# One in eight of the expert weights' low parts is computed on GpSimd instead of VectorE

## The chip, the cores and the metric

The kernel runs on one core of a Trainium2 chip. A core has TensorE (PE in the profile; PEld is its weight load), VectorE (DVE), ScalarE (ACT), GpSimd (POOL) and SyncE (SP), each with a queue of its own that it works off in order, and 16 DMA engines that move data between device memory and the core's on-chip memory SBUF. TensorE writes its results to eight banks of PSUM. The metric is the device time of one launch in microseconds (us); before the change it was 1439.66, the median of 3 runs from 1438.84 to 1440.0.

## The reference

Two transformer layers over 256 tokens of width 1024, in float32. Layer 0 is attention and a dense feed-forward block. Layer 1 is attention and a mixture of eight experts, of which each token uses two:

```python
def moe_swiglu(h, w_router, w1, w3, w2):
    t = h.reshape(b * s, d)
    logits = jnp.dot(t, w_router).astype(jnp.float32)
    top_val, top_idx = lax.top_k(logits, TOP_K)
    top_w = jax.nn.softmax(top_val, axis=-1)
    gates = jnp.einsum('tk,tke->te', top_w,
                       jax.nn.one_hot(top_idx, N_EXPERTS, dtype=jnp.float32)).astype(h.dtype)
    def expert(args):
        e_w1, e_w3, e_w2, g = args
        hid = jax.nn.silu(t @ e_w1) * (t @ e_w3)
        return (hid @ e_w2) * g[:, None]
    y = jnp.sum(lax.map(expert, (w1, w3, w2, gates.T)), axis=0)
```

For each expert e_w1 and e_w3 are 1024 x 3584 and e_w2 is 3584 x 1024. The change is in the experts.

## The kernel before

**Three products instead of one.** The matmuls here take float32r, not float32. So every weight w is split into a high part `wh` (w written as float32r) and a low part `wl` (w minus `wh`), and the tokens likewise; `mm3` (L174) then issues three matmuls into one bank: x_h·wh (L176), x_h·wl (L177), x_l·wh (L178). In the experts the tokens' parts `eh, el` lie in memory that the profile names `oh_t` and `ol_t`.

**The stream of weights.** All weights are loaded in one fixed order (`jobs`) by SP, 1 MB a tile (`raw`), into a ring of tile slots; a slot's next load starts when the slot's readers are done. `stream` (L138) hands the weights out. It takes half a tile at a time, 128 x 1024 numbers, called a *piece* below. ScalarE writes `wh` (L154), VectorE then writes `wl` from `raw` and `wh` (L155). The pool `split` (L52) has four buffers for `wh` and four for `wl`, so the two engines can be at most four pieces ahead of TensorE. A piece feeds six matmuls of 512 columns.

**The experts.** Tokens of an expert are gathered to at most 128 rows. An expert's hidden width is worked off in seven *blocks* of 512. A block takes four pieces of e_w1 into one bank, four pieces of e_w3 into another, and four pieces of e_w2 that go with the block before (L943 to L952). `gate_mul` (L584) makes `nat` = silu(w1 result) on ScalarE (L586), times the w3 result on VectorE (L587); `hid_t` (L592) turns `nat` by four transposes (L598) and splits it on ScalarE and VectorE (L182, L183). Each expert thus has 84 pieces, 7 `nat` and 7 splits of the turned hidden values. VectorE's queue holds all of them in one order, and so does ScalarE's.

**What GpSimd does before.** In the experts it only issues transfers, in order: four indirect DMAs that scatter the tokens to `xs_d` by expert (L828, during the first expert), a load of the next expert's tokens (L848) and a store of each expert's result (L855), and near the end some fetches (L836).

**Order.** The program is written in the order of the code below; a scheduler with its own timing model then sets the order within each engine's queue. It moves matmuls past others that it expects to wait.

Of the kernel before, what the change touches and what calls it, by code (L numbers as in the profile page):

```python
# [10 lines left out]
F32 = mybir.dt.float32  # L11
# [10 lines left out]
NC = D // P  # L22
# [15 lines left out]
WARM = 6  # L38
WARMS = 1, 1, 1
MIDDLE = 6  # L40
FAR = 4096
PUMPS = (7, 7), (7, 7), (7, 7), (7, 7), (2, 3), (2, 3), (1, 3), (2, 2), (2, 2)

# [2 lines left out]
def block_kernel(ctx: ExitStack, tc: tile.TileContext, x, w_qkv, w_o, mixer_norm, ffn_norm,  # L46
                 rel_bias, w1, w3, w2, router, e_w1, e_w3, e_w2, final_norm, onehot, out):
    nc = tc.nc
# [57 lines left out]
    def behind(*pairs):  # L106

        for a, b in pairs:
            if b is not None:
                tc.add_manual_dep(a.ins, b.ins.name,  # L110
                                  mybir.DependencyInfo(mybir.DependencyClass.NoSync,
                                                       mybir.DependencyReason.DATA),
                                  reason="issue order")

    held, recent = [None, None], [None]
# [18 lines left out]
    def load_ahead():  # L134
        while n_loaded[0] < min(n_used[0] + len(slots_of), len(jobs)):
            load_next()

    def stream(n, g=None, hold=(None, None), free=2):  # L138


        got = taken = 0
        while got < n:
            load_ahead()
            t = loaded[n_used[0]]
            _, nk, fn = jobs[n_used[0]]
            n_used[0] += 1
            k = min(nk, HALF // fn)
            for c0 in range(0, nk, k):
                wh = split.tile([P, HALF], F32R, name="wh")
                wl = split.tile([P, HALF], F32R, name="wl")  # L150
                m = k * fn
                src = t[:, c0 * fn:c0 * fn + m]
                if g is None:
                    i0 = nc.scalar.activation(wh[:, :m], src, AF.Copy)  # L154
                    i1 = nc.vector.tensor_sub(wl[:, :m], src, wh[:, :m].bitcast(F32))  # L155
                    if taken >= free:
                        behind((i0, hold[0]), (i1, hold[1]))
                else:
                    for c in range(k):
                        cs = slice(c * fn, (c + 1) * fn)  # L160
                        gc = gcol[:, g, got + c0 + c:got + c0 + c + 1]
                        i0 = nc.scalar.activation(wh[:, cs], src[:, cs], AF.Copy, scale=gc)  # L162
                        i1 = nc.vector.scalar_tensor_tensor(  # L163
                            wl[:, cs], src[:, cs], gc, wh[:, cs].bitcast(F32), op0=ALU.mult,
                            op1=ALU.subtract)
                        if taken >= free:
                            behind((i0, hold[0]), (i1, hold[1]))
                recent[0] = i0
                taken += 1
                for c in range(k):  # L170
                    yield wh[:, c * fn:(c + 1) * fn], wl[:, c * fn:(c + 1) * fn]
            got += nk
        assert got == n
# [116 lines left out]
    def norm_t(b, n, rms_too=True):  # L290
        for i in range(2):
            i0, i1 = split_out(turn(b, i),
                               xh[b][:, 4 * i:4 * i + 4].rearrange("p c t -> p (c t)"),
                               xl[b][:, 4 * i:4 * i + 4].rearrange("p c t -> p (c t)"))
        if rms_too:
            behind((rnorm(b, n), i0))
        return i0, i1
# [361 lines left out]
    hold = [norm_t(b, 0, False) for b in range(NB)]  # L659
# [4 lines left out]
    hold = hold[2:]  # L664
# [21 lines left out]
    def logits(b, after, between=None):  # L686
        lps = bank[0][:, b * NE:(b + 1) * NE]
        for c in range(NC):
            if c == MIDDLE and between:
                i0 = between()  # L690
# [125 lines left out]
    def send():  # L816

        nc.gpsimd.iota(rank, pattern=[[0, NB], [P, NE]], base=-1, channel_multiplier=0,
                       allow_small_or_imprecise_dtypes=True)
        nc.vector.tensor_scalar(place, slot, float(P), float(FAR), op0=ALU.is_gt, op1=ALU.mult)  # L820
        nc.vector.tensor_add(place, place, slot)
# [114 lines left out]
    for e in range(NE):  # L936
        for i, (f0, n) in enumerate(ecs):
            b1, b3 = (5, 6) if k % 2 == 0 else (3, 4)
            k += 1
            for bk in (b1, b3):  # L940
                if bk == b3:
                    held[:] = None, None
                for c, w in enumerate(stream(NC, hold=held)):  # L943
                    _, last = mm3(bank[bk], (eh[:, c], el[:, c]), w, c == 0, c == NC - 1)
                if pend is not None and bk == b1:
                    hT = hid_t(pend[1], FC, bank[pend[2]], *hts)
            if i == len(ecs) - 1 and e + 1 < NE:
                turn_x(xr, (2, 7), last)
            t = gate_mul(ep.tile([P, FC], F32, name="nat"), bank[b1], bank[b3], n)
            if pend is not None:  # L950
                for j, w in enumerate(stream(4)):
                    down(y, hT, j, w, pend[0] == 0, pend[0] == len(ecs) - 1)  # L952
            pend = (i, t, b1)
            if i == 0:
                if e:
                    store_y(e - 1)
                else:
                    gates()
                    send()

                    cps = bank[2]
                    for b in range(NB):
                        nc.tensor.matmul(cps[:, :NE], ones, sel[:, b], start=b == 0,
                                         stop=b == NB - 1)
                    most = mp.tile([P, 1], F32, name="most")
                    nc.vector.tensor_reduce(most, cps[:, :NE], axis=mybir.AxisListType.X,
                                            op=ALU.max)
                    most_i = mp.tile([P, 1], mybir.dt.int32, name="most_i")
                    nc.vector.tensor_copy(most_i, most)  # L969
                    nc.vector.tensor_scalar(pos2, slot, -float(P), None, op0=ALU.add)  # L970
            if i == 1 and e + 1 < NE:
                xr = load_x(e + 1)
            if e == NE - 1:
                if i == 0:
                    for b in range(NB):
                        mark(e, b)
                    done = slots(e)
                elif i == 2:
                    came = fetch(0, 0), fetch(0, 1)
                elif i == 3:  # L980
                    add_rows(0, came)
                    came = fetch(1, 0), fetch(1, 1)
                elif i == 4:
                    add_rows(1, came)
# [81 lines left out]
    for half in range(2):  # L1066
# [3 lines left out]
        i0, i1 = scatter(done, (half,), hts if half else ys)  # L1070
# [5 lines left out]
    for b in range(NB):  # L1076
# [3 lines left out]
        i1 = nc.vector.scalar_tensor_tensor(ms, ss[:, b, 1:2], 1.0 / D, ms, op0=ALU.mult,  # L1080
                                            op1=ALU.add)
# [49 lines left out]
```

## Time and profile before

| | |
|---|---|
| median of the runs | 1439.66 us |
| the profiled execution | 1440.46 us |
| its span on the core | 1438.7 us |
| TensorE busy | 1420.6 us (99%) |
| VectorE busy | 1170.3 us (81%) |
| ScalarE busy | 1009.7 us (70%) |
| GpSimd busy | 49.7 us (3%) |
| the 710 `wl` of L155 on VectorE | 834.1 us, 1221 ns each |
| the 710 `wh` of L154 on ScalarE | 724.7 us, 1056 ns each |

The experts fill the profile from about 457 us to 1424 us. Shares over the whole span mix stages: in the slices of the experts VectorE is at 9 tenths, in those of attention at 5 to 7. A busy TensorE is a modelled number (its matmuls are pipelined), so the start-to-start distance of matmuls tells more than its busy share. Idle time of an engine costs something only where another engine then waits for it.

### The profile page before, as it was taken

How to read it: one execution, taken by the hardware profiler on the slowest of the kernel's cores; microseconds unless marked ns; L12 is line 12 of the kernel's file. 1: busy time of each engine (PE TensorE's matmuls, PEld its weight loads, DVE VectorE, ACT ScalarE, POOL GpSimd, SP SyncE). 2: the span in 40 equal slices, each digit the busy share in tenths (PEclk: the TensorE clock that was granted, in tenths of full speed). 3: DMA queues.
4: the chain of work that ended last, by engine and by line, in shares of the span. 5: the costliest groups of instructions: out<-in, count | busy, mean ns of one | idle time of the engine just before them, and what ended most of it. 6: DMA issues, size and time to landing. Idle time of an engine off the chain costs nothing. (4 is left out here: it accounts for less than half of the span.)

```text
span 1438.7 us, 19644 instructions
## 1 busy us (share of the span) xinstructions
PE 1420.6 (99%) x7287; PEld 1179.9 (82%) x7287; DVE 1170.3 (81%) x1384; ACT 1009.7 (70%) x1282; POOL 49.7 (3%) x73
## 2 busy tenths in 40 slices
PE   9999999999999999999999999999999999999997
PEld 7877999988877888888888878878878888887785
DVE  6656666657766999999999988888888888888897
ACT  5656655546655888887887877777777777777775
POOL 1000000001001100000000000000000000001001
PEclk9999999999999999999999999999999999999998
DMA  9972855556575999999999999999999999999931
GB/s 343 190 259 89 304 194 190 191 176 228 169 254 198 397 397 378 392 377 373 394 368 378 385 361 371 371 382 371 359 384 369 369 373 377 364 368 375 368 140 57
DMA packets 172825, 445.23 MB, mean 309 GB/s; under 512 B 7299, under 2 KB 9379, under 8 KB 158644
## 3 DMA queue, kind: packets, MB, share of 16 engines
q1 hardware_dynamic: 166852, 422.61, 80.4%
q0 software_dynamic: 5808, 21.30, 5.4%
q8 instruction: 59, 0.97, 0.3%
q14 instruction: 42, 0.34, 0.1%
q10 hardware_dynamic: 64, 0.02, 0.0%
HBM read 430.00 MB, written 14.16 MB: 309 GB/s over the span
## 5 line engine op out<-in xcount | busy, mean ns | idle before, releaser
L155 DVE TENSOR_TENSOR wl<-raw,wh 128x1024 fp32r<-128x1024 f32 x710 | 834.1, 1221 | 113.3 <-ACT wh L154 106.8
L154 ACT ACTIVATE wh<-raw 128x1024 fp32r<-128x1024 f32 x710 | 724.7, 1056 | 131.2 <-PE bank L178 96.7
L177 PE MATMUL bank<-wl,oh_t 128*128 128x512 f32 x968 | 382.4, 396 | 2.3 <-DVE wl L155 2.2
L176 PE MATMUL bank<-wh,oh_t 128*128 128x512 f32 x968 | 374.6, 392 | 0.5 <-ACT oh_t L182 0.5
L178 PE MATMUL bank<-wh,oh_t 128*128 128x512 f32 x904 | 353.3, 391 | 0.0
L177 PEld LDWEIGHTS bank<-wl,oh_t 128*128 128x128 f32 x968 | 181.7, 188 | 59.1 <-DVE wl L155 19.4
L176 PEld LDWEIGHTS bank<-wh,oh_t 128*128 128x128 f32 x968 | 182.0, 188 | 39.3 <-ACT oh_t L182 0.9
L178 PEld LDWEIGHTS bank<-wh,oh_t 128*128 128x128 f32 x904 | 169.8, 188 | 33.5 <-DVE most_i L969 0.4
L178 PE MATMUL bank<-wh,ol_t 128*128 128x512 f32 x504 | 194.7, 392 | 0.0
L162 ACT ACTIVATE wh<-raw,gcol 128x512 fp32r<-128x512 f32 (+1 forms) x192 | 124.0, 699 | 88.7 <-PE bank L317 56.1
L163 DVE SCALAR_TENSOR_TENSOR wl<-raw,gcol,wh 128x512 fp32r<-128x512 f32 (+1 forms) x192 | 131.0, 725 | 66.8 <-ACT wh L162 66.4
L177 PE MATMUL bank<-wl,ol_t 128*128 128x512 f32 x440 | 175.0, 398 | 0.4 <-DVE wl L155 0.4
L317 PE MATMUL bank<-x_h,wh 128*128 128x256 f32 x512 | 144.0, 282 | 0.0
L317 PE MATMUL bank<-x_h,wl 128*128 128x256 f32 x512 | 143.0, 280 | 0.0
L317 PE MATMUL bank<-x_l,wh 128*128 128x256 f32 x512 | 142.9, 279 | 0.0
L176 PE MATMUL bank<-wh,ol_t 128*128 128x512 f32 x440 | 137.2, 393 | 0.0
L178 PEld LDWEIGHTS bank<-wh,ol_t 128*128 128x128 f32 x504 | 94.5, 188 | 19.8 <-issue 1.1
L317 PEld LDWEIGHTS bank<-x_h,wh 128*128 128x128 f32 x512 | 96.0, 188 | 1.9 <-issue 1.1
L177 PEld LDWEIGHTS bank<-wl,ol_t 128*128 128x128 f32 x440 | 83.1, 189 | 16.4 <-DVE wl L155 0.6
L317 PEld LDWEIGHTS bank<-x_h,wl 128*128 128x128 f32 x512 | 96.3, 188 | 0.0
L317 PEld LDWEIGHTS bank<-x_l,wh 128*128 128x128 f32 x512 | 96.0, 187 | 0.2
L176 PEld LDWEIGHTS bank<-wh,ol_t 128*128 128x128 f32 x440 | 81.6, 188 | 16.7
(221 smaller groups left out, 1120.6 us busy)
## 6 DMA issues: line engine op xcount, KB each, us to landing
raw<-in_e_w_dram SPq DMA_DIRECT2D x335, 1024.0 KB, 7.6
raw<-in_w_dram SPq DMA_DIRECT2D x33, 1024.0 KB, 5.1
raw<-in_w_qkv_dram SPq DMA_DIRECT2D x22, 1024.0 KB, 5.8
raw<-in_w_o_dram SPq DMA_DIRECT2D x8, 1024.0 KB, 12.9
xs_d<-hn POOLq DMA_DIRECT2D x1, 4096.0 KB, 15.9
xr<-xs_d POOLq DMA_DIRECT2D x7, 512.0 KB, 7.5
ys_d<-yr POOLq DMA_DIRECT2D x7, 512.0 KB, 7.8
rv_d<-rv POOLq DMA_DIRECT2D x1, 3072.0 KB, 36.4
```

The lines of the kernel that those rows point to most:

```text
L154: i0 = nc.scalar.activation(wh[:, :m], src, AF.Copy)
L155: i1 = nc.vector.tensor_sub(wl[:, :m], src, wh[:, :m].bitcast(F32))
L162: i0 = nc.scalar.activation(wh[:, cs], src[:, cs], AF.Copy, scale=gc)
L163: i1 = nc.vector.scalar_tensor_tensor(wl[:, cs], src[:, cs], gc, wh[:, cs].bitcast(F32), op0=ALU.mult, op1=ALU.subtract)
L176: i0 = nc.tensor.matmul(ps, s[0], m[0], start=start, stop=False)
L177: nc.tensor.matmul(ps, s[0], m[1], start=False, stop=False)
L178: i1 = nc.tensor.matmul(ps, s[1], m[0], start=False, stop=stop)
L317: nc.tensor.matmul(to, w[a][:, ms], z[:, :, c], start=c + i + m % 2 == 0, stop=c == NC - 1 and m % 2 == 1 and i == 2, skip_group_check=True)
```

## The change

`stream` gets an argument `aside`. Where it is set, a counter runs over the pieces, and of every eight pieces the fourth gets its `wl` from `nc.gpsimd.tensor_sub` instead of `nc.vector.tensor_sub`. It is set in all experts but for the first block of w1 and w3 and the last e_w2 block at the end: 660 pieces, of which 83 go to GpSimd. Since the pieces come in fours (w1, w3, w2), the piece that goes to GpSimd is always the last of its four: w1's and w2's last in one block, w3's last in the next.

```diff
@@ -38,6 +38,7 @@
+ASIDE = 8
@@ -135,7 +136,10 @@
-    def stream(n, g=None, hold=(None, None), free=2):
+    n_split = [0]
+
+    def stream(n, g=None, hold=(None, None), free=2, aside=0):
+
@@ -152,9 +156,15 @@
                     i0 = nc.scalar.activation(wh[:, :m], src, AF.Copy)
-                    i1 = nc.vector.tensor_sub(wl[:, :m], src, wh[:, :m].bitcast(F32))
                     if taken >= free:
-                        behind((i0, hold[0]), (i1, hold[1]))
+                        behind((i0, hold[0]))
+                    n_split[0] += aside
+                    if aside and n_split[0] % ASIDE == ASIDE // 2:
+                        nc.gpsimd.tensor_sub(wl[:, :m], src, wh[:, :m].bitcast(F32))
+                    else:
+                        i1 = nc.vector.tensor_sub(wl[:, :m], src, wh[:, :m].bitcast(F32))
+                        if taken >= free:
+                            behind((i1, hold[1]))
@@ -940,7 +950,7 @@
-                for c, w in enumerate(stream(NC, hold=held)):
+                for c, w in enumerate(stream(NC, hold=held, aside=e + i > 0)):
@@ -948,7 +958,7 @@
-                for j, w in enumerate(stream(4)):
+                for j, w in enumerate(stream(4, aside=True)):
```

Lines of the changed kernel are up to ten higher (L155 becomes L165 on VectorE and L163 on GpSimd, L176 to L178 become L186 to L188).

VectorE's queue in the middle of the experts, before and then changed, from one split of the turned hidden values (`ol_t`) on; `wl` are the pieces, `nat` the product with w3's result.

```order
L183 TENSOR_TENSOR ol_t<-bank_81,ol_t 128x512
L155 TENSOR_TENSOR wl<-raw,wh 128x1024 x8
L587 TENSOR_TENSOR nat<-nat,bank_80 128x512
L155 TENSOR_TENSOR wl<-raw,wh 128x1024 x4
L183 TENSOR_TENSOR ol_t<-bank_79,ol_t 128x512
```

```order
L193 TENSOR_TENSOR ol_t<-bank_81,ol_t 128x512
L165 TENSOR_TENSOR wl<-raw,wh 128x1024 x7
L597 TENSOR_TENSOR nat<-nat,bank_80 128x512
L165 TENSOR_TENSOR wl<-raw,wh 128x1024 x3
L193 TENSOR_TENSOR ol_t<-bank_79,ol_t 128x512
```

One or two pieces of the twelve in a block are gone from this queue; the rest keeps its order.

GpSimd's queue at the start of the experts, before and then changed: the scatter of the tokens to `xs_d`, then the first loads of an expert's tokens (`xr`).

```order
L818 IOTA rank 128x16
L828 DMA xs_d<-hn_147,row_in 1024x1024 x2
L828 DMA xs_d<-hn_148,row_in 1024x1024 x2
L848 DMA xr<-xs_d 128x1024 x2
L855 DMA ys_d<-yr 128x1024
```

```order
L828 IOTA rank 128x16
L838 DMA xs_d<-hn_147,row_in 1024x1024 x2
L838 DMA xs_d<-hn_148,row_in 1024x1024
L163 TENSOR_TENSOR wl<-raw,wh 128x1024
L838 DMA xs_d<-hn_148,row_in 1024x1024
L163 TENSOR_TENSOR wl<-raw,wh 128x1024
L858 DMA xr<-xs_d 128x1024
```

The first piece that GpSimd splits now stands behind three of the four scatters, the second behind the fourth.

TensorE's queue at the end of a w3 four in the middle of the experts, before and then changed; `bank_82` takes w3, `bank_76` and `bank_77` take w2.

```order
L176 MATMUL bank_82<-wh,oh_t 128x512
L177 MATMUL bank_82<-wl,oh_t 128x512
L178 MATMUL bank_82<-wh,oh_t 128x512
L176 MATMUL bank_82<-wh,oh_t 128x512
L177 MATMUL bank_82<-wl,oh_t 128x512
L178 MATMUL bank_82<-wh,oh_t 128x512
L176 MATMUL bank_76<-wh,ol_t 128x512
L176 MATMUL bank_77<-wh,ol_t 128x512
```

```order
L186 MATMUL bank_82<-wh,oh_t 128x512
L186 MATMUL bank_76<-wh,ol_t 128x512
L186 MATMUL bank_77<-wh,ol_t 128x512
L187 MATMUL bank_82<-wl,oh_t 128x512
L188 MATMUL bank_82<-wh,oh_t 128x512
L186 MATMUL bank_82<-wh,oh_t 128x512
L187 MATMUL bank_82<-wl,oh_t 128x512
L188 MATMUL bank_82<-wh,oh_t 128x512
```

The first matmul that needs GpSimd's `wl` (L187) now comes two matmuls later: the scheduler has put two of the next piece, which need only `wh`, ahead of it. At the end of a w1 or w2 four it is one matmul.

## Rows read from the trace of the kernel before

**Rows 1.** The page's costliest groups: two lines of `stream`.
```profile
L155 DVE TENSOR_TENSOR wl<-raw,wh 128x1024 fp32r<-128x1024 f32 x710 | 834.1, 1221 | 113.3 <-ACT wh L154 106.8
L154 ACT ACTIVATE wh<-raw 128x1024 fp32r<-128x1024 f32 x710 | 724.7, 1056 | 131.2 <-PE bank L178 96.7
```
**Rows 2.** Busy time of each engine in two experts' stretches.
```profile
core 0: us, PE busy (x) PEld busy (x) DVE busy (x) ACT busy (x) POOL busy (x), PEclk, DMA share, GB/s
684.30:803.10 118.80, 118.80 (x541) 98.82 (x540) 109.98 (x102) 96.03 (x102) 1.07 (x2) 1.00 1.02 379
1045.70:1167.30 121.60, 121.42 (x541) 97.83 (x540) 107.58 (x102) 91.93 (x102) 1.05 (x2) 1.00 1.01 371
```
**Rows 3.** Waits in 1052 to 1167 us: us in total, times, longest us.
```profile
ACT ol_t L182 <- PE bank L177: 11.3, 6, 1.9
DVE wl L155 <- ACT wh L154: 9.5, 14, 1.3
PEld bank L177 <- DVE wl L155: 3.6, 9, 0.6
```
**Rows 4.** Timeline at 446 us: start, us, engine, line, tiles, idle before.
```profile
446.71 0.55 POOL L277 TENSOR_TENSOR rms<-ms,mhalf 128x1 f32<-128x1 f32 x1 [0.61 <-DVE ms L276]
447.23 2.52 POOL L728 TENSOR_TENSOR hn<-hn,gain 128x512 f32<-128x512 f32 x2
448.43 1.85 DVE L725 SCALAR_TENSOR_TENSOR hn<-h,rms,gain 128x512 f32<-128x512 f32 x1
451.85 0.75 DVE L725 SCALAR_TENSOR_TENSOR hn<-h,rms,gain 128x512 f32<-128x512 f32 x1
```
**Rows 5.** Timeline of GpSimd and VectorE at 1408 us.
```profile
1408.35 1.31 POOL L989 TENSOR_SCALAR oh_t<-ident 128x128 fp32r<-128x128 f32 x1
1409.42 1.31 DVE L155 TENSOR_TENSOR wl<-raw,wh 128x1024 fp32r<-128x1024 f32 x1
```
**Rows 6.** Timeline of one block in the sixth expert: ScalarE, VectorE, TensorE.
```profile
1051.93 3.89 ACT L154 ACTIVATE wh<-raw 128x1024 fp32r<-128x1024 f32 x4
1057.65 4.91 ACT L154 ACTIVATE wh<-raw 128x1024 fp32r<-128x1024 f32 x5
...
1053.01 4.63 DVE L155 TENSOR_TENSOR wl<-raw,wh 128x1024 fp32r<-128x1024 f32 x4 [0.26 <-ACT wh L154]
1058.74 4.63 DVE L155 TENSOR_TENSOR wl<-raw,wh 128x1024 fp32r<-128x1024 f32 x4 [1.10 <-ACT wh L154]
1063.88 4.63 DVE L155 TENSOR_TENSOR wl<-raw,wh 128x1024 fp32r<-128x1024 f32 x4
...
1054.29 0.51 PE L177 MATMUL bank<-wl,oh_t 128*128 128x512 f32 x1
1055.80 0.39 PE L177 MATMUL bank<-wl,oh_t 128*128 128x512 f32 x1
1056.03 0.40 PE L178 MATMUL bank<-wh,oh_t 128*128 128x512 f32 x1
1061.53 0.39 PE L177 MATMUL bank<-wl,oh_t 128*128 128x512 f32 x1
1066.25 0.47 PE L177 MATMUL bank<-wl,ol_t 128*128 128x512 f32 x1
```
**Rows 7.** Timeline of one block in the third expert: ScalarE, TensorE.
```profile
707.60 3.07 ACT L154 ACTIVATE wh<-raw 128x1024 fp32r<-128x1024 f32 x3
...
711.22 0.39 PE L177 MATMUL bank<-wl,oh_t 128*128 128x512 f32 x1
```
**Rows 8.** Timeline in the first expert: GpSimd's third scatter, and TensorE.
```profile
473.96 2.90 POOL L828 DMA_INDIRECT xs_d<-hn,row_in  x1 [7.34 <-DMA xs_d<-hn,row_in]
...
473.63 0.39 PE L177 MATMUL bank<-wl,oh_t 128*128 128x512 f32 x1
```
**Rows 9.** Busy time and granted clock in two stretches around 450 us.
```profile
450.00:451.00 1.00, 0.26 (x1) 0.26 (x2) 0.93 (x6) 0.00 (x0) 0.00 (x0) 0.50 0.33 117
456.00:458.00 2.00, 2.00 (x14) 1.63 (x12) 1.26 (x10) 1.02 (x2) 0.00 (x0) 0.87 0.31 71
```

## The prediction

> **What bounds the kernel now.** I read the page first (what is costly), then busy time by expert, then the waits of one expert of each kind, then the timelines of single blocks. The page shows the `wl` and `wh` pieces as the costliest lines of VectorE and ScalarE [rows 1]; that says nothing yet about what they hold up. Busy time by expert does: an early expert takes 118.8 us and TensorE is busy in all of it, while VectorE works 109.98 us; a later one takes 121.6 us with VectorE at 107.58 [rows 2]. So in the early kind (the first three experts) TensorE is the bound and VectorE has some 9 us to spare; the later kind (the other five) is 2.8 us longer with a VectorE that works less. The waits tell why: TensorE's weight load waits 3.6 us for `wl`, in 9 short waits, VectorE waits 9.5 us for `wh`, ScalarE 11.3 us for TensorE [rows 3]. The later kind loses time to a loop (TensorE, ScalarE, VectorE, TensorE) in which every engine in turn waits in order, not to a VectorE with too much work.
>
> The block in rows 6 shows how tight that loop is. ScalarE makes four `wh` from 1051.93, VectorE follows from 1053.01 with four `wl`, and TensorE starts on the first of them at 1054.29, when VectorE has just finished it (1053.01 + 1.22 = 1054.23). That matmul shows 0.51 us where its neighbours show 0.39: a wait costs about 0.11 us more than itself. In an early block there is more room: a `wh` ready at 707.60 + 1.06 = 708.66 [rows 1, 7] is needed as `wl` only at 711.22.
>
> **The change part by part.**
>
> *VectorE is rid of 83 pieces.* Back to back a piece takes (4.63 - 1.22) / 3 = 1.14 us [rows 1, 6]; 83 x 1.14 = 94 us of work go, 10.4 pieces or 11.8 us an expert. On TensorE, which sets the time in the early kind, this gives nothing. In the later kind the most it could give is the 2.8 us an expert, if `wl` were what is late; but the pieces that are just in time wait for `wh`, and ScalarE keeps its work.
>
> *GpSimd gets them.* No piece of this form is in the trace. The nearest rows are GpSimd's two subtract-like products of 128x512 numbers, together the same count: 2.52 us [rows 4]. Take 2.5. Above, 2.54 is the two without overlap; below, if the 0.55 us that GpSimd needs for a single column [rows 4] were all fixed cost, 2.52 - 0.55 = 1.97.
>
> *VectorE stands still meanwhile.* In rows 4 VectorE's L725, two inputs in SBUF, takes 1.85 us beside GpSimd's product and 0.75 alone: it started at 448.43 and ended 0.53 us after GpSimd's second product (449.75), as if it could only begin to stream there. The other way round, GpSimd's L989 took 1.31 us for 128x128 numbers, beginning just after a VectorE piece, and the next piece took 1.31 instead of 1.22 [rows 5]: GpSimd waited for the piece under way and then went first. The Trainium skill says this as a rule ("SBUF — State Buffer", "Who interferes with whom"): a VectorE instruction with two SBUF inputs and a GpSimd instruction that reads SBUF exclude each other for a whole instruction, whichever began first. The trace agrees, with 1.10 us lost by L725. The Trainium skill in another place ("Advanced Engine Details and Errata", "VectorE Performance Modes") names only VectorE's two-port modes as the conflict and gives two-input operations none; by that there would be no exclusion, which is a rival below.
>
> So each of the 10.4 pieces an expert takes 1.14 us off VectorE and puts 2.5 on it: +14.1 us. Early kind: 109.98 + 14.1 = 124.1 us of work in 118.8. Some of it closes up when VectorE never pauses (84 tails of 0.08 us, at most 6.7; and `nat` and `ol_t`, which read PSUM, may run beside GpSimd), so between +0 and +5.3 us an expert. A single GpSimd piece just about fits: 708.66 + 2.5 = 711.16 against 711.22 [rows 7]. I take +2.5, in the middle, for three experts: **+7**.
>
> *Later kind.* Two positions of the GpSimd piece matter, both in rows 6, each about 3.5 times an expert. Last of w1: four `wh` in 3.89 us are (3.89 - 1.06) / 3 = 0.94 apart, so its `wh`, the second, is ready at 1051.93 + 0.94 + 1.06 = 1053.93; VectorE is on the piece before until 1053.01 + 1.14 = 1054.15; GpSimd then ends at 1056.65. TensorE wants it at 1055.80, or, with the one matmul that now goes ahead (0.23 us, the step to the next row), at 1056.03: late by 0.62, with the restart 0.73. Last of w3: VectorE's piece from 1058.74 ends its streaming at 1059.88, GpSimd ends at 1062.38, wanted at 1061.53 + 0.45 = 1061.98: 0.40 late, 0.51 with the restart. Last of w2: at 1063.88 VectorE begins the piece before; if it is first, GpSimd ends at 1065.02 + 2.5 = 1067.5, before its turn, which is six matmuls after 1066.25. I cost it at nothing; the cover is that VectorE goes first. If GpSimd goes first, VectorE's piece ends at 1063.88 + 2.5 + 1.22 = 1067.6 instead of by 1066.25: 1.35 late. Sum: 3.5 x (0.73 + 0.51) = 4.3 us an expert, 5 experts, **+22**. Bounds: with 1.97 us the delays are 0.09 and none, 3.5 x 0.20 = 0.7, so +4; with 1.35 in each w2 turn another 4.7, so +45. VectorE's work would be 107.6 + 14.1 = 121.7 in 125.9, so it isn't the bound there.
>
> *GpSimd's queue in the first expert.* The first GpSimd piece stands behind the third scatter, which is issued at 473.96 after 7.34 us of waiting for the transfer before it and holds GpSimd until 476.86 [rows 8]. Then 2.5 us: `wl` at 479.4. TensorE wants it at 473.63 [rows 8]: 5.7 us of standstill, and four buffers don't let anything run ahead of it for long. After an idle stretch TensorE's granted clock was 0.50 at 450 to 451, and only back on the way up (0.87) in 456 to 458 [rows 9]; some 6 us at half speed do 3 us of work less. **+9** (0 if the transfers land earlier; 5.7 without the clock; 12 if it falls for longer). The second piece, behind the fourth scatter, is wanted only later than that. The other transfers of GpSimd's queue stand between pieces that are blocks apart.
>
> *The rest.* The loads of `raw` wait for its readers, now GpSimd too; ScalarE has no wait for a load among those of rows 3, and a slower TensorE asks for less. No cost.
>
> Sum: 7 + 22 + 9 = 38 on the profiled execution's 1440.46 (span 1438.7), 1478.5. The median of the runs is 0.8 lower than that execution, so **1478**.
>
> **Rivals.**
>
> *GpSimd goes first at the wrong time.* Wherever it takes the port just before an earlier piece, VectorE's next one is late. It decides when a GpSimd piece's `wh` is ready before VectorE has begun the piece before, as by a few hundredths at 1063.88. For: VectorE would be nearly full. Against: TensorE's own stops let it catch up. Then +45 for the later kind, 5.3 x 3 = 16 for the early, 12: 1440 + 73 = 1513.
>
> *No exclusion:* the two engines work side by side. (The Trainium skill's "Advanced Engine Details and Errata", "VectorE Performance Modes", would have it so.) The GpSimd pieces still are slow: 1053.93 + 2.5 = 1056.43 against 1056.03, 0.51 with restart; 1059.65 + 2.5 = 1062.15 against 1061.98, 0.28: 3.5 x 0.79 = 2.8 an expert, 14 in all, none in the early kind, 9 at the start: 1463. Against: rows 4.
>
> *Faster: the relieved VectorE ends the later experts' loss.* Place: the just-in-time pieces of rows 6. It needs a GpSimd piece in under 1056.03 - 1054.15 = 1.88 us, below my lower bound, and that VectorE, not ScalarE, is what those pieces wait for. Then 5 x 2.8 = 14 back, with the start hidden: 1426; with it 1435. For: VectorE is above 90% busy in the early kind. Against: it pauses more in the kind that is slower.
>
> *Nothing seen:* 1.97 us a piece, no queue at the start, delays filled from the slack: 1440 to 1444.
>
> **How the numbers follow.** Forecast 0.60, GpSimd first 0.14, no exclusion 0.11, faster 0.07, nothing seen 0.08. The forecast's own low end: 4 + 0 + 5.7 = 10, 1450. Range 1450 to 1513: it leaves out the faster and unseen cases and the far end of the first rival. A measurement of this kernel tells 0.2% (2.9 us) from no change: faster 0.07, within 0.2% 0.07, slower 0.86.
>
> **What the profile would show.** GpSimd's pieces at 2.4 to 2.6 us, more where they wait for VectorE; VectorE pieces of up to 2.5 + 1.2 us beside them (plain 1.22 everywhere means no exclusion); TensorE waits for GpSimd's `wl` some 40 times, 0.4 to 0.8 us, in the later five experts, 125 to 127 us each, and one wait of over 5 us near 474 us, with a lower granted clock behind it; early experts 120 to 122 us. I am wrong if the later experts get shorter, if there is no wait near 474, or if most waits are for VectorE's pieces.

## The result, and the profile after

The changed kernel takes 1477.09 us (median of 4 runs, 1474.04 to 1480.16) where the kernel before takes 1439.83: 1.0255 times as long, 95% interval 1.0235 to 1.0275, slower. The forecast was 1478 in a range of 1450 to 1513. The profiled execution took 1475.35 us, its span is 1473.2 us, 34.5 longer than before; its part ahead of the experts happened to be 2.65 us shorter, so 37.1 us were lost from the first expert on. One execution of each of two kernels below (2842.45 us where GpSimd only writes, 2345.52 with both holds from the second expert on) was far slower than the others of its kernel and is left out of their medians and ranges.

The page's costliest groups, to be held against [rows 1]:

```profile
L165 DVE TENSOR_TENSOR wl<-raw,wh 128x1024 fp32r<-128x1024 f32 x627 | 844.8, 1390 | 161.7 <-ACT wh L158 159.5
L163 POOL TENSOR_TENSOR wl<-raw,wh 128x1024 fp32r<-128x1024 f32 x83 | 216.9, 2613 | 658.8 <-ACT wh L158 657.4
```

VectorE has 83 pieces fewer and is busy in this line 10.7 us longer (834.1 before): its pieces went from 1221 to 1390 ns. So 627 x 0.169 = 106 us of standstill were added, 1.28 us for each of the 83 pieces of GpSimd, which take 2.61 us themselves on average.

Busy time of each engine in the stretches of the third and the fifth expert (columns as in [rows 2]), which were 118.8 and 121.6 us long before:

```profile
693.09:816.22 123.13, 120.13 (x543) 98.95 (x542) 107.31 (x92) 95.43 (x102) 27.72 (x13) 1.00 1.00 368
941.53:1067.96 126.43, 124.27 (x544) 97.69 (x543) 111.87 (x90) 92.23 (x102) 31.12 (x14) 1.00 0.99 358
```

VectorE is not full in either: 107.3 of 123.1 us, 111.9 of 126.4, standstill included. The waits in the second of these stretches (columns as in [rows 3]):

```profile
DVE wl L165 <- ACT wh L158: 14.0, 21, 2.2
ACT ol_t L192 <- PE bank L187: 10.7, 6, 2.2
ACT nat L596 <- PE bank L188: 10.3, 6, 2.2
PEld bank L187 <- POOL wl L163: 4.7, 7, 0.8
PEld bank L187 <- DVE wl L165: 4.4, 10, 0.6
```

The weight load's waits for `wl` are 9.1 us where they were 3.6 [rows 3]. VectorE waits longer for `wh` than before (14.0 against 9.5 us), and ScalarE stands for TensorE six times each at `ol_t` and `nat` in the stretch's seven blocks.

The weight load's waits for `wl` in the whole run, before and then changed:

```profile
PEld bank L177 <- DVE wl L155: 20.0, 46, 1.1
```

```profile
PEld bank L187 <- DVE wl L165: 34.3, 57, 2.1
PEld bank L187 <- POOL wl L163: 27.0, 33, 5.0
```

The 46 before all lie in the later five experts. In the changed kernel these five have 48 for VectorE's pieces (23.8 us) and 32 for GpSimd's (22.0 us), so what was added there is nearly all GpSimd's. Of the 32, 15 are for the last piece of w1 (12.2 us), 17 for the last of w3 (9.7 us) and none for the last of w2. The first three experts, which had no such wait before, have nine for VectorE's pieces (10.5 us), each for the first piece of w3, and one for GpSimd's.

The first GpSimd piece, first GpSimd and TensorE, then the granted clock (the column after the POOL count), to be held against [rows 8, 9]:

```profile
471.64 0.97 POOL L838 DMA_INDIRECT xs_d<-hn,row_in  x1 [8.50 <-DMA xs_d<-hn,row_in]
472.62 2.37 POOL L163 TENSOR_TENSOR wl<-raw,wh 128x1024 fp32r<-128x1024 f32 x1
...
469.83 0.48 PE L186 MATMUL bank<-wh,oh_t 128*128 128x512 f32 x1
475.04 0.66 PE L187 MATMUL bank<-wl,oh_t 128*128 128x512 f32 x1 [4.73 <-POOL wl L163]
```

```profile
470.00:474.00 4.00, 0.31 (x2) 0.00 (x0) 2.20 (x3) 0.96 (x2) 2.35 (x2) 1.00 0.67 272
474.00:476.00 2.00, 0.96 (x3) 0.77 (x4) 0.00 (x0) 0.00 (x0) 1.27 (x2) 0.80 0.23 92
476.00:478.00 2.00, 2.00 (x6) 1.58 (x5) 0.00 (x0) 0.49 (x1) 0.71 (x1) 0.50 0.97 274
478.00:480.00 2.00, 2.00 (x9) 1.57 (x8) 1.23 (x1) 1.83 (x3) 0.00 (x0) 0.84 0.96 303
```

TensorE stands 4.73 us, and when it starts again the granted clock is at its lower level (0.50) and back at 1.00 by 480: 0.20 x 2 in 474 to 476, 0.50 x 2 in 476 to 478 and 0.16 x 2 in 478 to 480, 1.7 us of work not done.

An early expert (the second), about the last piece of w1, which is now GpSimd's: GpSimd, ScalarE, VectorE, TensorE.

```profile
681.69 2.40 POOL L163 TENSOR_TENSOR wl<-raw,wh 128x1024 fp32r<-128x1024 f32 x1 [9.23 <-ACT wh L158]
...
680.06 0.60 ACT L192 ACTIVATE ol_t<-bank 128x512 fp32r<-128x512 f32 x1 [0.80 <-PE bank L187]
680.56 2.00 ACT L158 ACTIVATE wh<-raw 128x1024 fp32r<-128x1024 f32 x2
...
682.59 3.73 DVE L165 TENSOR_TENSOR wl<-raw,wh 128x1024 fp32r<-128x1024 f32 x2 [1.03 <-ACT wh L158]
...
685.23 0.50 PE L187 MATMUL bank<-wl,oh_t 128*128 128x512 f32 x1 [0.65 <-DVE wl L165]
```

GpSimd's own piece is in time (684.09). VectorE's next one, the first of w3, begins at 682.59 and stands until GpSimd ends: its two pieces take 3.73 us where they would take 1.14 + 1.22 = 2.36, so the first ends at 682.59 + 3.73 - 1.14 = 685.18, and TensorE, which wanted it at 684.58, begins at 685.23. Ahead of all this ScalarE stood 0.80 us at `ol_t` with one piece of w1 still to make.

A later expert (the sixth), at the same place: ScalarE, GpSimd, TensorE.

```profile
1108.16 0.60 ACT L192 ACTIVATE ol_t<-bank 128x512 fp32r<-128x512 f32 x1 [1.95 <-PE bank L187]
1108.65 3.89 ACT L158 ACTIVATE wh<-raw 128x1024 fp32r<-128x1024 f32 x4
1114.74 0.60 ACT L596 ACTIVATE nat<-bank 128x512 f32<-128x512 f32 x1 [2.20 <-PE bank L188]
...
1110.73 2.50 POOL L163 TENSOR_TENSOR wl<-raw,wh 128x1024 fp32r<-128x1024 f32 x1 [9.40 <-ACT wh L158]
...
1113.28 0.49 PE L187 MATMUL bank<-wl,oh_t 128*128 128x512 f32 x1 [0.35 <-POOL wl L163]
```

Here GpSimd's piece itself is late: ScalarE stands 1.95 us at `ol_t` with two pieces of w1 still to make, GpSimd gets the second of the four `wh` that follow and ends at 1113.23, TensorE restarts 0.05 later. Then ScalarE stands 2.20 us at `nat`, again two pieces before the end of a four, this time w3's.

Where the 37.1 us lie, read from the issue times of the loads of the next expert's tokens in both traces: first expert 8.2 (from the writing of `rank`, the last step ahead of it, on), second and third 3.2 and 4.4, the fourth to the eighth 4.3, 4.8, 3.7, 4.9 and 3.6, the end included in the last.

### The profile page after: what moved, and what is told of

The parts are those of the page before. It is cut to its first block, busy times and chain, and to the rows that moved or that the text cites. A ratio compares the mean times of both kernels' runs of the same rounds, so it can differ in the third digit from the quotient of the medians.

```text
span 1473.2 us, 19712 instructions
## 1 busy us (share of the span) xinstructions
PE 1434.3 (97%) x7287; PEld 1175.7 (80%) x7287; DVE 1180.8 (80%) x1301; ACT 1009.5 (69%) x1282; POOL 264.2 (18%) x156
## 5 line engine op out<-in xcount | busy, mean ns | idle before, releaser
L165 DVE TENSOR_TENSOR wl<-raw,wh 128x1024 fp32r<-128x1024 f32 x627 | 844.8, 1390 | 161.7 <-ACT wh L158 159.5
L187 PE MATMUL bank<-wl,oh_t 128*128 128x512 f32 x968 | 388.2, 402 | 24.4 <-POOL wl L163 10.8
L186 PE MATMUL bank<-wh,oh_t 128*128 128x512 f32 x968 | 373.3, 394 | 0.5 <-ACT oh_t L192 0.5
L188 PE MATMUL bank<-wh,oh_t 128*128 128x512 f32 x904 | 354.0, 392 | 0.4 <-DVE most_i L979 0.4
L163 POOL TENSOR_TENSOR wl<-raw,wh 128x1024 fp32r<-128x1024 f32 x83 | 216.9, 2613 | 658.8 <-ACT wh L158 657.4
L187 PEld LDWEIGHTS bank<-wl,oh_t 128*128 128x128 f32 x968 | 181.9, 188 | 99.2 <-DVE wl L165 34.3
L186 PEld LDWEIGHTS bank<-wh,oh_t 128*128 128x128 f32 x968 | 182.2, 188 | 39.9 <-ACT oh_t L192 0.9
L188 PEld LDWEIGHTS bank<-wh,oh_t 128*128 128x128 f32 x904 | 170.2, 188 | 32.6 <-DVE most_i L979 0.8
L188 PE MATMUL bank<-wh,ol_t 128*128 128x512 f32 x504 | 194.7, 392 | 0.0
L187 PE MATMUL bank<-wl,ol_t 128*128 128x512 f32 x440 | 175.2, 398 | 0.0
L186 PE MATMUL bank<-wh,ol_t 128*128 128x512 f32 x440 | 136.8, 392 | 0.0
L188 PEld LDWEIGHTS bank<-wh,ol_t 128*128 128x128 f32 x504 | 94.4, 188 | 19.3 <-issue 1.1
L187 PEld LDWEIGHTS bank<-wl,ol_t 128*128 128x128 f32 x440 | 83.1, 189 | 16.4
```

Of the source, the lines that this page charges most:

```text
L163: nc.gpsimd.tensor_sub(wl[:, :m], src, wh[:, :m].bitcast(F32))
L186: i0 = nc.tensor.matmul(ps, s[0], m[0], start=start, stop=False)
L187: nc.tensor.matmul(ps, s[0], m[1], start=False, stop=False)
L188: i1 = nc.tensor.matmul(ps, s[1], m[0], start=False, stop=stop)
```

## The experiments

All were timed beside the kernel before; its median in the three groups of runs was 1439.54, 1440.0 and 1440.5 us. Edits are cut to the lines that matter, and `...` marks a cut. How long single experts took (the distance of two such loads) is in a table further down.

### VectorE keeps all pieces, GpSimd makes the 83 again

```diff
...
-                        nc.gpsimd.tensor_sub(wl[:, :m], src, wh[:, :m].bitcast(F32))
-                    else:
-                        i1 = nc.vector.tensor_sub(wl[:, :m], src, wh[:, :m].bitcast(F32))
...
+                        nc.gpsimd.tensor_sub(spare[0][:, :m], src, wh[:, :m].bitcast(F32))
+                    i1 = nc.vector.tensor_sub(wl[:, :m], src, wh[:, :m].bitcast(F32))
...
```

Expected: 

> VectorE makes all 710 low parts again, as in the kernel before; GpSimd computes the same 83 differences a second time into a spare tile that nothing reads (the ring of weight tiles has one slot fewer to make room). So TensorE never waits for GpSimd's result, and only what GpSimd does to VectorE is left. Theory (the two exclude each other while both read two tiles from SBUF): VectorE stands still for about 2.4 us 83 times, 10.4 x 2.4 = 25 us an expert on top of its 108 to 110, so it becomes the bound of every expert at 128 to 135 us: 1510 to 1560 us, with VectorE pieces of up to 3.6 us in the trace. Rival (no exclusion, the changed kernel lost only by the late GpSimd piece): 1440 to 1444 us, and VectorE pieces of 1.22 us throughout.

Measured: 1558.39 us (1555.33 to 1560.17), ratio 1.0814 (1.0774 to 1.0854). TensorE waits for no GpSimd piece here, yet the kernel is 119 us slower. The three lines of its trace:

```profile
L164 DVE TENSOR_TENSOR wl<-raw,wh 128x1024 fp32r<-128x1024 f32 x710 | 992.4, 1453 | 90.3 <-ACT wh L158 89.6
L163 POOL TENSOR_TENSOR spare<-raw,wh 128x1024 fp32r<-128x1024 f32 x83 | 256.4, 3089 | 687.9 <-ACT wh L158 459.9 <-issue 152.3 <-DMA raw<-in_e_w_dram 62.3
L158 ACT ACTIVATE wh<-raw 128x1024 fp32r<-128x1024 f32 x710 | 719.1, 1055 | 191.4 <-PE bank L187 127.1 <-POOL spare L163 29.2 <-PE bank L326 22.8
```

VectorE's piece goes from 1221 to 1453 ns, 710 x 0.232 = 165 us, 1.98 for each GpSimd piece. The two engines exclude each other. The Trainium skill states this, for a VectorE instruction with two SBUF inputs and a GpSimd instruction that reads SBUF, in "SBUF — State Buffer", "Who interferes with whom", and the trace agrees, with the 1453 ns. The length of the pieces shows it, the 119 us do so less: ScalarE also waits 29.2 us until GpSimd has read a `wh`, which it doesn't do in the changed kernel's trace.

### GpSimd only writes

```diff
...
+                        nc.gpsimd.tensor_copy(spare[0][:, :1], wh[:, :1].bitcast(F32))
+                        for f in (HALF, HALF, HALF // 2):
+                            nc.gpsimd.memset(spare[0][:, :f].bitcast(F32), 0.0)
...
```

in place of the difference that GpSimd makes in the kernel above.

Expected: 

> Like the run with the spare tile, but in place of each second difference GpSimd copies one column of wh (so that it starts at the same moment) and then fills the spare tile with zeros, 2.5 x 1024 numbers a row, some 2.4 us in which it writes SBUF and reads nothing. Theory (it is GpSimd's reading that excludes VectorE's two-input pieces): no standstill, VectorE's pieces stay at 1.22 us but for about 0.1 us beside the one-column copy: 1440 to 1446 us. Rival (any GpSimd instruction on SBUF excludes them): 1510 to 1560 us, as with the spare differences.

Measured: 1446.4 us (median of nine runs, 1442.56 to 1450.03), ratio 1.0041 (1.0021 to 1.0061). GpSimd is as busy as with the differences (202.7 us of filling and 53.0 us of one-column copies, against 256.4), and VectorE's piece is what it was before:

```profile
L166 DVE TENSOR_TENSOR wl<-raw,wh 128x1024 fp32r<-128x1024 f32 x710 | 832.9, 1221 | 114.3 <-ACT wh L158 109.4
L165 POOL MEMSET spare<- 128x1024 f32 (+1 forms) x249 | 202.7, 814 | 14.5
L163 POOL CAST spare<-wh 128x1 fp32r<-128x1 f32 x83 | 53.0, 639 | 584.9 <-ACT wh L158 584.9
```

So it is GpSimd's reading that excludes, not that it works or writes. The 6 us that remain lie in the later experts (122.9 instead of 121.6); what makes them was not looked into. Two things differ here besides: the ring of loads has one slot fewer than before, as in the kernel above, and ScalarE's queue takes the order of the later kind three blocks earlier, before the third expert ends.

### GpSimd takes half a piece, twice as often

```diff
-ASIDE = 8
+ASIDE = 4
...
-                    if aside and n_split[0] % ASIDE == ASIDE // 2:
-                        nc.gpsimd.tensor_sub(wl[:, :m], src, wh[:, :m].bitcast(F32))
+                    if aside and n_split[0] % ASIDE == 0:
+                        d = m // 2
+                        nc.vector.tensor_sub(wl[:, :d], src[:, :d], wh[:, :d].bitcast(F32))
+                        nc.gpsimd.tensor_sub(wl[:, d:m], src[:, d:], wh[:, d:m].bitcast(F32))
```

Expected: 

> GpSimd takes the second half (512 of 1024 columns) of the last piece of every four, VectorE the first half: the same numbers on GpSimd in all, in 166 instructions of about 1.25 us. Theory (in the later five experts the loss is the late piece): the low part is there 1.2 us sooner, inside the slack of the last piece of w1 and of w3, so those experts fall back to about 121 to 123 us; the wait at the start stays (about 6 us), the early three lose 1 to 3 us each where GpSimd goes first: 1447 to 1462 us. Rival (the loss is VectorE's standstill, which in sum is the same 2.4 us per eight pieces and a little more for twice the instructions): 1473 to 1483 us, as the changed kernel.

Measured: 1480.85 us (1478.4 to 1481.9), ratio 1.0278 (1.0244 to 1.0313). A miss. The halves don't run beside each other (GpSimd, then VectorE):

```profile
1000.78 1.38 POOL L165 TENSOR_TENSOR wl<-raw,wh 128x512 fp32r<-128x512 f32 x1 [4.64 <-ACT wh L158]
...
1000.92 1.78 DVE L164 TENSOR_TENSOR wl<-raw,wh 128x512 fp32r<-128x512 f32 x1
```

VectorE's half ends at 1002.70, 0.54 after GpSimd's: one after the other, 1.9 us for the piece in place of 1.2, at the last of every four instead of every second. The early experts lose nothing at all by it (118.78, with VectorE busy for 109.8 us), the later ones up to 8.4 (130.1). That contradicts a VectorE that is full in the early kind. In the later kind a smaller delay at twice as many places costs more than the whole pieces did; the run doesn't tell the places apart.

### Only from the second expert on

```diff
-                for c, w in enumerate(stream(NC, hold=held, aside=e + i > 0)):
+                for c, w in enumerate(stream(NC, hold=held, aside=e > 0)):
-                for j, w in enumerate(stream(4, aside=True)):
+                for j, w in enumerate(stream(4, aside=e > 0)):
```

Expected: 

> The change as it is, but from the second expert on: in the first expert VectorE makes all low parts, so no piece stands between the scatters in GpSimd's queue. Theory (the start costs on its own: a wait of 4.7 us, the lower clock after it, and the first expert's share of the early kind's loss, 8 us in all in the trace of the changed kernel): 1467 to 1471 us. Rival (the wait at the start is filled from what the engines have ahead and costs nothing in the end): 1475 to 1479 us.

Measured: 1466.97 us (1466.64 to 1467.69), ratio 1.018 (1.0146 to 1.0215), at the theory's lower end. 10.1 us of the loss went with the first expert's pieces, where the traces showed 8.2.

### ScalarE's order fixed, in the kernel before and in the changed one

`ol_t` in ScalarE's queue stands ahead of the last piece of w1 in the first three experts and ahead of its last two in nearly all blocks of the other five; `nat` stands behind the last of w3 in the first three and ahead of its last two in nearly all blocks of the others. ScalarE works in order, so it can't fill free buffers with `wh` while it stands there. This edit holds both behind the last `wh` that is written before them in the program, in the experts only:

```diff
...
-            nc.scalar.activation(t[:, :n], p1[:, :n], AF.Silu)
+            behind((nc.scalar.activation(t[:, :n], p1[:, :n], AF.Silu), late[0] and recent[0]))
...
-        split_out(ps[:, :n], a[:, :n], c[:, :n])
+        i0, _ = split_out(ps[:, :n], a[:, :n], c[:, :n])
+        behind((i0, late[0] and recent[0]))
...
```

Expected of the kernel before with it: 

> The kernel before (no piece on GpSimd), with ScalarE's order fixed in the experts: the Silu of `nat` is issued behind the last `wh` of w3 and the copy of `ol_t` behind the last `wh` of w1, so that ScalarE no longer stands in order on TensorE for them while the next four `wh` could be made. Theory (what makes the later five experts longer is the loop TensorE, ScalarE, VectorE, TensorE, closed by ScalarE standing some 20 us an expert in order at `nat` and `ol_t`): later experts fall from 121.6 to about 118.8 us, time about 1426, at the furthest 1424. Rival (the loop does not pass through these two waits; the buffers set it): 1437 to 1442. Third: the moved copies come later than TensorE wants them: 1445 or more.

Expected of the changed kernel with it: 

> The changed kernel with the same fixed order of ScalarE. Theory (the later experts pay 3.7 to 4.9 us each for GpSimd's pieces because every piece there is just in time; with ScalarE's order fixed the pieces have the slack of the early kind and pay like it, some 3 us): with the later experts at 121 to 123 us, time 1455 to 1462. Rival (VectorE's standstill behind 10.4 pieces an expert sets the cost, whatever the slack): the 37 us remain on top of the order's gain or loss, so the time of the kernel before with fixed order plus 34 to 40.

Measured: the kernel before 1431.16 us (1430.43 to 1435.02, 5 runs), ratio to itself without the edit 0.9942 (0.9928 to 0.9956); the changed kernel 1436.2 us (1433.3 to 1438.51, 10 runs), ratio to the kernel before 0.997 (0.9957 to 0.9983). So the change costs 5 us there instead of 37, and with the edit even the changed kernel is 0.3% faster than the kernel before. Neither expectation was met in its number: the first gained 9 us, not 14, the second far more than the theory gave it. In the kernel before with fixed order ScalarE no longer stands at either (ScalarE in the sixth expert, from an execution of 1434.99 us, 3.8 above the median):

```profile
1048.57 1.06 ACT L154 ACTIVATE wh<-raw 128x1024 fp32r<-128x1024 f32 x1 [0.53 <-PE bank L178]
1049.54 0.58 ACT L182 ACTIVATE ol_t<-bank 128x512 fp32r<-128x512 f32 x1
...
1053.78 1.06 ACT L154 ACTIVATE wh<-raw 128x1024 fp32r<-128x1024 f32 x1 [0.30 <-PE bank L178]
1054.75 0.58 ACT L586 ACTIVATE nat<-bank 128x512 f32<-128x512 f32 x1
```

It waits at the `wh` instead, for one of the four buffers to come free. In the changed kernel with fixed order, the fifth expert's busy times, its waits of the weight load (all of them), and the page's line of GpSimd's pieces:

```profile
926.99:1046.72 119.73, 119.56 (x544) 99.11 (x542) 108.28 (x91) 95.84 (x103) 29.87 (x14) 1.00 1.01 380
```

```profile
PEld bank L187 <- POOL wl L163: 0.6, 1, 0.6
```

```profile
L163 POOL TENSOR_TENSOR wl<-raw,wh 128x1024 fp32r<-128x1024 f32 x83 | 214.7, 2587 | 618.4 <-ACT wh L158 617.6 <-issue 0.8
```

GpSimd's pieces are as long as in the changed kernel (2587 against 2613 ns), VectorE's are still stretched (1357 ns on average, 1390 in the changed kernel), and TensorE hardly notices. What made them cost was where ScalarE stood.

### One of the two held

Expected with `nat` alone: 

> The changed kernel with only the Silu of `nat` held behind the last `wh` of w3 (in the later experts ScalarE otherwise reaches it two pieces before that); `ol_t` stays where it was, one piece before the last of w1 in the early experts and two before it in the later ones. Theory (each of the two stands of ScalarE exposes the GpSimd piece behind it: `ol_t` that of w1, `nat` that of w3): the later experts keep w1's share, 3.5 x 0.73 = 2.6 us, and lose w3's 1.8 and up to 1.4 of the loop; early ones and start unchanged: 1461 to 1468. Rival (`nat` alone carries the later experts' cost): early experts and start remain, 1450 to 1458. Other rival (`ol_t` alone): 1474 to 1479.

Expected with `ol_t` alone: 

> The changed kernel with only the copy of `ol_t` held behind the last `wh` of w1, in all experts; `nat` stays two pieces before the last of w3 in the later experts and behind it in the early ones. Theory: early experts repaired (118.3 to 119 us, 10 us less), later experts lose w1's 2.6 us and keep w3's 1.8 and part of the loop, start unchanged: 1447 to 1456. Rival (`ol_t` alone carries it): 1434 to 1442. Other rival (`nat` alone carries the later experts' cost): 1464 to 1469, from the early experts alone.

Measured: `nat` alone 1458.16 us (1457.66 to 1459.72), ratio 1.0122 (1.0101 to 1.0142), between what the theory and its first rival gave; `ol_t` alone 1455.35 (1454.99 to 1458.78), ratio 1.011 (1.0087 to 1.0134), as the theory had it. The two gains add up: (1477.1 - 1458.2) + (1477.1 - 1455.4) = 18.9 + 21.7 = 40.6, and both together gave 1477.1 - 1436.2 = 40.9. `nat` is worth 3.7 to 3.8 us in each of the fourth to the seventh expert and nothing in the first three; `ol_t` 2.2 to 3.7 in each from the second to the seventh and nothing in the first.

| us, from the trace of | 2nd | 3rd | 4th | 5th | 6th expert |
|---|---|---|---|---|---|
| the kernel before | 118.8 | 118.8 | 121.0 | 121.6 | 121.7 |
| before, order fixed | 118.8 | 118.3 | 118.8 | 120.7 | 120.7 |
| the changed kernel | 122.0 | 123.1 | 125.3 | 126.4 | 125.4 |
| changed, `nat` held | 121.9 | 123.1 | 121.5 | 122.8 | 121.6 |
| changed, `ol_t` held | 118.3 | 121.0 | 122.0 | 123.6 | 122.5 |
| changed, both held | 118.3 | 121.0 | 118.5 | 119.7 | 118.5 |
| changed, second of a four | 119.0 | 118.8 | 121.8 | 121.3 | 122.3 |
| changed, half pieces | 118.8 | 118.8 | 126.1 | 130.1 | 130.1 |

### Both held, from the second expert on

The edits of "ScalarE's order fixed" and of "Only from the second expert on" together.

Expected: 

> The changed kernel with both held, and GpSimd's pieces only from the second expert on. Theory (the 5.0 us by which the changed kernel with fixed order is behind the kernel before with fixed order, 1436.2 against 1431.2, are the standstill of 3.7 us behind the third scatter in the first expert and the clock behind it; no other GpSimd piece costs anything): 1430 to 1433, no difference to the kernel before with fixed order. Rival (the 5 us lie spread over the experts, as VectorE's standstills): 1435 to 1438.

Measured: 1429.3 us (median of four runs, 1428.87 to 1432.62), ratio 0.9927 (0.9905 to 0.995), as the theory had it but for 0.7 us. What is left of the change's cost with a fixed order is the start: 1436.2 - 1429.3 = 6.9 us. There the changed kernel with fixed order shows a standstill at the same place:

```profile
475.01 0.50 PE L187 MATMUL bank<-wl,oh_t 128*128 128x512 f32 x1 [3.67 <-POOL wl L163]
```

The 74 pieces that GpSimd still makes cost nothing that shows, and gain nothing that shows: the ranges of this kernel and of the kernel before with fixed order overlap. In the traces its third expert is 2.7 us longer (121.0 against 118.3) and its fourth to seventh are 0.2 to 2.2 us shorter. But the other trace is the one of 1434.99 us, so whether the later experts gain by GpSimd's pieces is not shown.

### Another place for GpSimd's piece

```diff
-                    if aside and n_split[0] % ASIDE == ASIDE // 2:
+                    if aside and n_split[0] % ASIDE == 2:
```

The second piece of a four in place of the last, with ScalarE's order left to itself.

Expected: 

> The changed kernel, with GpSimd on the second piece of a four in place of the last; number and size of GpSimd's pieces as before. Theory (it is a late piece at a place without slack that costs, and the last of w1 and of w3 are the worst places): the second of w1 has slack, the second of w2 and w3 are 0.2 to 0.4 us late, so the later experts pay about 2 us less each and the first GpSimd piece comes earlier behind the scatter: 1465 to 1472. Rival (the sum of VectorE's standstills decides, not the place): 1474 to 1480. Third (VectorE's own later pieces of the same four are now behind the standstill and are late each time): 1483 or more.

Measured: 1449.15 us (1448.54 to 1453.9), ratio 1.0062 (1.0046 to 1.0077): 28 us less than the changed kernel, and a miss, 16 less than the theory's lower end. As many pieces, somewhat longer ones (2688 ns on average), and the experts from the second on are within 0.9 us of those before (table). The start remains (4.3 us of standstill for a GpSimd piece). The weight load still waits for GpSimd's pieces in the experts (21 times, 17.7 us, the start's included), but less for VectorE's (23 times, 10.0 us). In the later experts the second of w1 lies ahead of ScalarE's `ol_t` and the second of w3 is the fourth piece behind it, ahead of `nat`; the last of w1 and the last of w3 are each the second piece behind one of the two. So it isn't the number of GpSimd's pieces or their length that costs, but that a slow piece comes close behind a standstill of ScalarE.

### Six buffers instead of four

```diff
-RING1, RING2, RING3 = 1, 3, 3
+RING1, RING2, RING3 = 1, 3, 1
...
+        splits.extend([split] * 3 + [ctx.enter_context(pool)] * 2)
```

Expected: 

> The changed kernel with six buffers for `wh` and `wl` in the experts in place of four (the ring of loads a little shorter to make room). Theory (in the early experts VectorE is not full; each GpSimd piece only delays the VectorE piece behind it past TensorE's turn, and two more buffers let it be made earlier): early experts back from 122 to 123 us to about 119, start unchanged, later ones 1 to 3 us better: 1460 to 1470. Rival (VectorE is full there, as the prediction's 124.1 us of work has it): early experts stay at 122 or more, 1474 to 1480.

Measured: 1485.39 us (1483.27 to 1488.83), ratio 1.0323 (1.0307 to 1.0338). Neither theory nor rival. The second and third expert came to 120.0 and 123.3 us, the fourth to the seventh to 127.9 to 130.3. The scheduler also put `ol_t` and `nat` elsewhere in ScalarE's queue (in the first experts one right behind the other), and ScalarE stands longer at both (570 to 1300 us of its trace, where the changed kernel has 49.0 and 42.9):

```profile
ACT ol_t L195 <- PE bank L190: 93.5, 26, 4.9
ACT nat L599 <- PE bank L191: 59.5, 36, 5.1
```

With the ring of loads, which is two slots shorter here, three things changed at once, and the run decides nothing on VectorE; it fits the reading that ScalarE's standstills set the time.

## Why the prediction was right, and where only its number was

**The sum: right, in part by luck.** The later kind was put at 22 us and cost 21.3. The start was put at 9 and cost 6.4, the early kind at 7 and cost 9.4: these two errors cancel, and the early kind's number rests on a mechanism that the runs don't bear out (below).

**Exclusion: right.** VectorE's pieces of up to 3.36 us, and the two kernels in which GpSimd makes the differences again or only writes (pieces of 1453 against 1221 ns, 1558.4 against 1446.4 us) leave nothing to the rival without exclusion.

**GpSimd's piece at 2.5 us: right.** 2.37 to 3.39, median 2.50; 2.8 to 3.39 in every third piece of the later kind, the last of w2, where it waits for VectorE first. This is the cover that the forecast gave for costing w2 at nothing, and none of these pieces was waited for.

**VectorE's load: wrong.** That each piece "takes 1.14 us off VectorE and puts 2.5 on it" counted the whole of GpSimd's piece as VectorE's standstill. Measured it was 1.28 us a piece, about what was taken off: the rest of each falls into time in which VectorE pauses anyway, as 0.90 of the 2.40 us do in the rows of the early expert above. Its 124.1 us of work in an early expert came to 107.3.

**Early kind, +7: the number near (3.2 and 4.4 in two experts, some 2 of the first's 8.2), the mechanism wrong.** VectorE wasn't full. The late piece is the one behind GpSimd's, once in two blocks by 0.65 us, because `ol_t` stands ahead of w1's last `wh`: with `ol_t` held the second expert is back at 118.3, with nearly as much standstill on VectorE (its pieces there are stretched by 9.1 us in all, 10.9 in the changed kernel). About 2.5 us of the third expert (the changed kernel with `ol_t` held still takes 121.0 there) are something else, which the prediction dismissed with "the other transfers of GpSimd's queue stand between pieces that are blocks apart". One does not: GpSimd issues a store of an expert's result just ahead of a piece that is ready (GpSimd and TensorE in the changed kernel with both held).

```profile
711.81 0.56 POOL L866 DMA_DIRECT2D ys_d<-yr  x1 [9.65 <-ACT ol_t L192]
712.39 2.42 POOL L163 TENSOR_TENSOR wl<-raw,wh 128x1024 fp32r<-128x1024 f32 x1
...
715.96 0.50 PE L187 MATMUL bank<-wl,oh_t 128*128 128x512 f32 x1 [1.47 <-DVE wl L165]
```

**Later kind, +22: right in size (21.3) and in place, with a cause behind it that was not told.** The two positions, last of w1 and last of w3, are where it was lost (0.81 and 0.57 us a wait of the weight load, where 0.73 and 0.51 had been worked out), and leaving them (second of a four) took the loss away. The prediction took ScalarE's waits as a given part of a loop and rows 3 as proof that later pieces must be just in time. They are so only because of the order of ScalarE's queue: with the two holds the same GpSimd pieces cost nothing that shows in these experts, and the kernel before loses some of its own 2.8 us too. That GpSimd's slower piece comes late there was true of this order alone.

**Start, +9: right in kind, too large.** 4.7 us of standstill and 1.7 of clock, 6.4 in the trace, 6.9 between the two kernels with fixed order. The scatter held GpSimd 0.97 us here and not 2.90, and the granted clock was back by 480.

**The faster rival** needed a GpSimd piece below 1.88 us, and none was. Its other condition, that VectorE is what the later experts wait for, is not borne out either: with GpSimd's pieces at another place, where they cost almost nothing, these experts are no shorter than before.

**The signs.** The later experts (125.3 to 126.4 us) and the wait near 474 us came as told, but for 4.73 us in place of over 5; the third expert, at 123.1, is above the 120 to 122. One sign of being wrong came too: most waits in the later experts are for VectorE's pieces, 48 against 32. It was badly chosen, as 46 of these were there before; what was added is GpSimd's. In the early kind, where all the waits but one are VectorE's, the sign is right: that mechanism was the wrong one.

**What stays open.** In the trace of the kernel before with fixed order two of the three later experts in the table still take 120.7 us, 2 more than the third. Why was not tried; the executions of this kernel fall into two groups, three at 1430.4 to 1431.2 us and two at 1435.0, and the trace is of one of the latter. What makes the 6 us of the kernel in which GpSimd only writes was not tried either.

## What to carry to other kernels

Work that is given to a slower engine costs by the place of its pieces: put them where the consumer is several pieces away, never just behind a point at which an in-order queue stands and waits for that consumer. Before an engine is relieved, look at which queue stands still in order with free buffers behind it; here two holds on ScalarE brought 9 us, and giving away pieces of VectorE brought nothing that shows even where it cost nothing. An engine that is 90% busy in a stage need not be its bound: look whether it still waits for its producer there.

## What the runs showed that was not expected

GpSimd doesn't always get its turn at the end of the VectorE piece under way. In the kernel with the doubled pieces ten of the 83 took 6.0 to 7.5 us. The longest, beside VectorE pieces back to back (GpSimd, VectorE):

```profile
600.77 7.48 POOL L163 TENSOR_TENSOR spare<-raw,wh 128x1024 fp32r<-128x1024 f32 x1 [3.34 <-ACT wh L158]
...
599.11 6.89 DVE L164 TENSOR_TENSOR wl<-raw,wh 128x1024 fp32r<-128x1024 f32 x6
605.92 0.67 DVE L596 TENSOR_TENSOR nat<-nat,bank 128x512 f32<-128x512 f32 x1
```

VectorE's six pieces went undisturbed (6.89 / 6 = 1.15 us each), and GpSimd ended 2.33 us after VectorE had turned to `nat`, which reads PSUM: it had stood through all that were left of them. In 16 other places (a piece of 3.2 to 3.5 us) it waited for about one VectorE piece, and 52 took at most 2.6 us; what decides between these isn't shown.

And a standstill of TensorE of 4.7 us cost another 1.7 us by the granted clock, less than the 3 us that were worked out from [rows 9].
